# A decoder trunk on one core: sums of x in the first v pass, gate weights loaded during the second, gate bias added by VectorE, and other slots between the stages

## The chip, the core and the metric

The kernel runs on one core of a Trainium2 chip. Its engines are TensorE (PE; its weight loads are shown as PEld), VectorE (DVE), ScalarE (ACT), GpSimd (POOL) and SyncE (SP), which here only issues transfers. Each engine takes its instructions in program order, and semaphores order them between engines. The metric is the device time of one execution in microseconds (us), as the median of several.

## The reference, cut to what matters

One layer of a decoder trunk on x of 512 tokens by 2048 features, in float32:

```python
h = x @ w_in + b_in      # columns: [FoX q,k,v,z,forget | SWA q,k,v,z | MoBA q,k,v,z | gates fox,swa,moba]
# A: attention with a running sum of log_sigmoid(forget), 8 heads of 64
# B: sliding-window attention, window 128, a learned sink per head
# C: attention to the own block of 256 and the best past blocks
branch_i = (heads_i * silu(z_i)) @ w_branch_i           # 512 -> 2048, for A, B and C
y   = sum_i sigmoid(gate_i) * branch_i                  # three gates of 2048 columns each
out = layer_norm(alpha * x + y @ w_out)
```

## The kernel before, in words

Every matrix product is made of three TensorE products of reduced-precision parts: an operand is split into `hi` (a rounded copy, by ACT) and `lo` (the rest, `raw - hi`, by DVE; the helper `split` or `lower`), and hi*hi, lo*hi and hi*lo are summed in PSUM. Weights come by transfer from SP into `raw` tiles, are split two steps ahead of their matmuls, and there are three pairs of `hi` and `lo`. DVE and ACT do this for every step, in one order with everything else that the program gives them.

The order of all work is the order in which the program is written. The stages follow each other on PE:

1. The v projection (`v_step`, L234): two passes of 16 steps over x's 16 row blocks, each step 12 matmuls of 324 columns, into the PSUM tiles `va` and `vc`. In the first pass each x block is loaded (`load_x`) and split into `xh` and `xl`, which stay in SBUF. `v_evac` adds the bias `vb` and stores the result to `v_rows`.
2. For the gates, `x_sums` forms for eight pairs of x blocks four sums each on POOL (`s1raw`, `xsum`); `x_sums_split` and `s1_split` split them into `sh`/`sl` and into a part of `xh`/`xl`.
3. The gate projection: six groups (three gates, two halves each) by a fast scheme of seven products instead of eight. A group has 56 steps (seven products of eight), `gate_step` (L333), each six matmuls of 512 columns into `alpha`, `beta` and `gamma`, two tiles of each. The weights are four quarters a, b, c and d, four blocks each; the dictionary `LOADS` says at which step of a group the next group's blocks are asked for, and `COMBINE` at which step DVE adds or subtracts quarters in place (`rawb = rawc - rawb`, and so on). `gate_post` takes the sums out of PSUM; its `finish` adds the gate's bias on POOL, and the sigmoid and the store to `gate_tiles` follow three steps later.
4. The h projection: steps of 12 matmuls (L727 to L729), for q, k and z of the heads, with the attention's work put between the steps by `at(i, order, f)`: f is run in step i, sorted by `order`. Before the first head, `v_split` splits v from `v_rows`, `forget_bias` forms the log-sigmoid terms (`t0` to `pair`) from `flog`, and `running_sum` sums them on PE (`csum`). `q_lower` (L548) takes a q tile from PSUM. `nsink` is the negated sink, from `sinkc`.
5. The branch products `br` (L859) of the split head outputs `ozh`/`ozl` (`split_oz`), the product with the gates, the transposes `yt` (`turn_y`, L888), the output product `o` (L918 to L920) and the layer norm. `late_gate` and `late_silu` take the last z tiles from PSUM.

The places in the first v pass and the attention that the change moves are these, before:

```python
        if KD - 1 <= n < KD + 7:
            pend[n] = x_sums(n - KD + 1)
...
    for st in range(4):
        for ps in range(2):
            at(st, 3, v_split, ps, st, fox_dests[ps])
    nl = {}
    at(4, 4, lambda: nl.update(n=forget_bias()))
    at(6, 8, lambda: running_sum(nl["n"]))
```

Of the kernel before, what the change touches and what calls it, by code (L numbers as in the profile page):

```python
# [87 lines left out]
def hybrid_kernel(ctx: ExitStack, tc: tile.TileContext, a: dict, out: bass.AP):  # L88
# [155 lines left out]
    for n in range(2):  # L244
        prepare_v(n)
    pend = {}
    gate_loads = {}
    for n in range(2 * KD):
        if n + 4 < KD:
            load_x(n + 4)  # L250
        if n % 2 == 0 and n // 2 + 3 < KD:
            load_v(n // 2 + 3)
        if n + 2 < 2 * KD:
            prepare_v(n + 2)
        if n == KD:
            vacc[1] = [att_tile(f"vc{i}") for i in range(4)]
        if KD - 1 <= n < KD + 7:
            pend[n] = x_sums(n - KD + 1)
        v_step(n)
        if KD <= n < KD + 8:  # L260
            x_sums_split(n - KD, pend[n - 1])
        if n >= KD + 2 and n % 2 == 0:
            s1_split((n - KD - 2) // 2)
        if KD + 1 <= n < KD + 5:
            v_evac(0, n - KD - 1)
    x_ctx.close()


    rawp = gate_ctx.enter_context(tc.tile_pool(name="rawp", bufs=4))
    raw_of = {}  # L270

    def load_gate(sc, q, blk):
        if sc >= len(GROUPS):
# [6 lines left out]
        nc.sync.dma_start(r, a["wa"][(sc * 4 + "abcd".index(q)) * 4 + blk])  # L280
# [66 lines left out]
    def finish(sc, t, i, n, u):

        b, half = GROUPS[sc]
        nc.gpsimd.tensor_tensor(out=t, in0=t, in1=evs[sc, "bias", n], op=ALU.add)  # L350
# [7 lines left out]
    def gate_post(sc, m):

        out = []  # L360
        if m == 6:
            for n in range(2):
                evs[sc, "bias", n] = post.tile([P, S], F32, tag="bias", name="gbias")
                nc.gpsimd.dma_start(evs[sc, "bias", n], a["bg"][2 * sc + n:2 * sc + n + 1].to_broadcast([P, S]))
        elif m in (7, 8):
            u = m - 7
            nc.scalar.activation(post_tile(sc, "p1", "p", u), bank(sc, "alpha", u), AF.Copy)
        elif m in (15, 16):
            u = m - 15
            nc.vector.tensor_add(post_tile(sc, "u2", "u", u), bank(sc, "beta", u), evs[sc, "p1", u])  # L370
        elif m in (23, 24):
            u = m - 23
            nc.scalar.activation(post_tile(sc, "c11", "c", u), bank(sc, "alpha", u), AF.Copy)
            out.append(finish(sc, evs[sc, "c11", u], 0, 0, u))
        elif m in (31, 32):
            u = m - 31
            nc.vector.tensor_add(post_tile(sc, "u3", "c", u), bank(sc, "beta", u), evs[sc, "p1", u])
        elif m in (39, 40):
            u = m - 39
            t = evs[sc, "u3", u]  # L380
            nc.vector.tensor_add(t, bank(sc, "gamma", u), t)
            out.append(finish(sc, t, 1, 1, u))
        elif m in (47, 48):
            u = m - 47
            t = evs[sc, "p1", u]
            nc.vector.tensor_add(t, bank(sc, "beta", u), t)
            out.append(finish(sc, t, 1, 0, u))
        elif m in (55, 56):
            u = m - 55
            t = evs[sc, "u2", u]  # L390
            nc.vector.tensor_add(t, bank(sc, "gamma", u), t)
            out.append(finish(sc, t, 0, 1, u))
        return out
# [32 lines left out]
    gate_ahead(0)  # L426
    gate_ahead(1)
    for n in range(items):
# [7 lines left out]
        for f in later.pop(n, ()):
            f()
        if m == 0 and sc:
            later.setdefault(n + 3, []).extend(gate_post(sc - 1, 56))
        later.setdefault(n + 3, []).extend(gate_post(sc, m))  # L440
# [5 lines left out]
    tail = gate_post(len(GROUPS) - 1, 56)  # L446
    for n in sorted(later):
        for f in later[n]:
            f()
    for f in tail:  # L450
        f()
    gate_ctx.close()


    ozy = ctx.enter_context(tc.tile_pool(name="ozy", bufs=12))
# [1 line left out]
    work = att_ctx.enter_context(tc.tile_pool(name="work", bufs=2))
    const = att_ctx.enter_context(tc.tile_pool(name="const", bufs=1))
    flog = const.tile([P, 4, NH], F32, name="flog")
    vfox = const.tile([P, 4, NH, P], F32R, tag="v", name="vfox")  # L460
    vswa = const.tile([P, 4, 2, P], F32R, name="vswa")
    sinkc = const.tile([P, NH], F32, name="sinkc")
    nsink = const.tile([P, NH], F32, name="nsink")
    vld = [work.tile([P, 4, NV], F32, tag="pth", name=f"vld{j}") for j in range(2)]
    for j in range(2):
        nc.sync.dma_start(vld[j], a["vs"][j])
    nc.gpsimd.dma_start(sinkc, a["sinks"].to_broadcast([P, NH]))
# [639 lines left out]
```

## Time and profile before

| | |
|---|---|
| median of three runs | 1398.51 us (1398.47 to 1399.36) |
| the profiled execution | 1399.42 us |
| its span in the profile | 1397.7 us |
| granted TensorE clock, mean | 0.984 |
| PE busy | 1343.8 us (96%) |
| DVE busy | 925.2 us (66%) |
| ACT busy | 655.7 us (47%) |
| POOL busy | 264.2 us (19%) |
| moved by DMA | 174.97 MB, mean 125 GB/s |

The span is that of the profiled execution; 1.7 us of its time lie outside it. The clock is the share of full speed that the chip granted to PE; where PE has waited, the profile shows stretches of half clock. A list of waits gives, for an engine and a line, what it waited for. `L` numbers are those of the kernel before.

### The profile page before, as it was taken

What the parts mean: (1) busy time and instruction counts of PE and PEld (TensorE: products, weight loads), DVE (VectorE), ACT (ScalarE), POOL (GpSimd) and SP (SyncE); (2) the same over time, 40 slices, a digit from 0 to 9 for tenths busy, and PEclk for the clock granted to TensorE, in tenths of its full rate; (3) what the DMA queues carried; (4) which work ended last, traced back from release to release, by engine and by line L of the source; (5) the groups of instructions that cost most, each with busy time, mean ns of one, the idle gap of its engine ahead of it and who ended that gap; (6) DMA issues with size and microseconds to landing.
All of it is one profiled execution on the core that took longest, in us unless ns stands there. A gap on an engine that the chain in (4) does not pass through costs nothing.

```text
span 1397.7 us, 18535 instructions
## 1 busy us (share of the span) xinstructions
PE 1343.8 (96%) x6435; PEld 1122.3 (80%) x6435; DVE 925.2 (66%) x1591; ACT 655.7 (47%) x1202; POOL 264.2 (19%) x300
## 2 busy tenths in 40 slices
PE   8889999999999999899999999999998999999994
PEld 7868788787878788688888998888887888888884
DVE  5758888898888888556666556555645666533348
ACT  4435555455555555456655555565653222222231
POOL 3601311122121311212122323121220000000006
PEclk9899999999999999999999999999999999999998
DMA  7271707153351703342222222222224555543223
GB/s 234 84 274 41 259 33 260 42 212 105 128 188 37 261 34 101 135 121 85 97 91 78 82 76 91 76 76 91 76 76 166 181 181 181 191 170 105 91 76 120
DMA packets 57822, 174.97 MB, mean 125 GB/s; under 512 B 6568, under 2 KB 8104, under 8 KB 56960
## 3 DMA queue, kind: packets, MB, share of 16 engines
q1 hardware_dynamic: 47680, 150.07, 32.3%
q10 hardware_dynamic: 8064, 13.91, 2.6%
q0 software_dynamic: 1984, 9.81, 2.2%
q8 instruction: 50, 0.82, 0.2%
q14 instruction: 44, 0.36, 0.1%
HBM read 155.64 MB, written 18.12 MB: 124 GB/s over the span
## 4 chain that ended last, share of the span: by engine, by line
PE 82%; DVE 7%; issue 4%; DMA 3%; POOL 1%; ACT 1%; SPq 0%; DVEq 0%; ACTq 0%; POOLq 0%
PE h L727 9%; PE h L729 9%; PE h L728 8%; PE br L859 8%; PE beta L341 4%; PE o L918 4%; PE o L919 4%; PE o L920 4%; PE beta L339 4%; PE beta L340 4%; PE alpha L341 3%; PE gamma L339 3%; PE gamma L340 3%; PE gamma L341 3%; DVE glo L116 2%
## 5 line engine op out<-in xcount | busy, mean ns | idle before, releaser
L144 ACT ACTIVATE hi<-raw 128x512 fp32r<-128x512 f32 x252 | 158.8, 631 | 334.8 <-PE o L919 107.0
L147 DVE TENSOR_TENSOR lo<-raw,hi 128x512 fp32r<-128x512 f32 x252 | 177.4, 707 | 170.4 <-ACT hi L144 140.1
L727 PE MATMUL h<-xh,hi 128*128 128x512 f32 x528 | 208.9, 396 | 3.9 <-ACT hi L144 3.9
L729 PE MATMUL h<-xh,lo 128*128 128x512 f32 x528 | 207.4, 393 | 2.0 <-DVE lo L147 2.0
L728 PE MATMUL h<-xl,hi 128*128 128x512 f32 x528 | 206.7, 391 | 0.0
L643 POOL TENSOR_SCALAR lt<-lt,st 128x128 f32<-128x128 f32 (+2 forms) x96 | 71.2, 741 | 295.7 <-DVE st L642 293.8
L729 PEld LDWEIGHTS h<-xh,lo 128*128 128x128 f32 x528 | 99.5, 188 | 24.9 <-DVE lo L147 3.3
L727 PEld LDWEIGHTS h<-xh,hi 128*128 128x128 f32 x528 | 99.5, 189 | 22.7 <-ACT hi L144 4.3
L728 PEld LDWEIGHTS h<-xl,hi 128*128 128x128 f32 x528 | 99.7, 189 | 18.8
L116 DVE TENSOR_TENSOR glo<-rawd,ghi 128x512 fp32r<-128x512 f32 x96 | 74.8, 779 | 33.1 <-ACT ghi L115 27.6
L115 ACT ACTIVATE ghi<-rawa 128x512 fp32r<-128x512 f32 x96 | 59.2, 630 | 68.7 <-DVE rawa L308 29.0
L115 ACT ACTIVATE ghi<-rawd 128x512 fp32r<-128x512 f32 x96 | 60.7, 633 | 63.2 <-DVE glo L116 37.7
L918 PE MATMUL o<-hi,yh 128*128 128x512 f32 (+1 forms) x232 | 88.9, 383 | 0.7 <-DVE z L924 0.7
L919 PE MATMUL o<-hi,yl 128*128 128x512 f32 (+1 forms) x232 | 88.6, 382 | 0.0
L341 PE MATMUL alpha<-glo,xh 128*128 128x512 f32 x192 | 77.6, 404 | 11.4 <-DVE glo L116 10.7
L115 ACT ACTIVATE ghi<-rawb 128x512 fp32r<-128x512 f32 x96 | 60.6, 633 | 59.5 <-PE beta L340 23.7
L920 PE MATMUL o<-lo,yh 128*128 128x512 f32 (+1 forms) x232 | 88.6, 382 | 0.0
L116 DVE TENSOR_TENSOR glo<-rawb,ghi 128x512 fp32r<-128x512 f32 x96 | 75.9, 821 | 8.0 <-PE alpha L340 4.0
L859 PE MATMUL br<-hi,ozh 128*128 128x512 f32 x192 | 76.3, 398 | 4.5 <-ACT ozh L115 4.5
L341 PE MATMUL beta<-glo,sh 128*128 128x512 f32 x192 | 76.1, 396 | 1.2 <-DVE glo L116 1.2
L339 PE MATMUL alpha<-ghi,xh 128*128 128x512 f32 x192 | 76.2, 397 | 1.0 <-ACT ghi L115 1.0
L340 PE MATMUL alpha<-ghi,xl 128*128 128x512 f32 x192 | 75.8, 395 | 0.0
(229 smaller groups left out, 3191.3 us busy)
## 6 DMA issues: line engine op xcount, KB each, us to landing
raw<-in_ws SPq DMA_DIRECT2D x130, 512.0 KB, 3.5
rawc<-in_wa SPq DMA_DIRECT2D x25, 512.0 KB, 4.4
rawa<-in_wa SPq DMA_DIRECT2D x24, 512.0 KB, 5.0
rawb<-in_wa SPq DMA_DIRECT2D x24, 512.0 KB, 5.8
rawd<-in_wa SPq DMA_DIRECT2D x24, 512.0 KB, 5.4
sig<-gate_tiles SPq DMA_DIRECT2D x48, 256.0 KB, 3.9
gate_tiles<-u ACTq DMA_DIRECT2D x24, 256.0 KB, 4.0
rawv<-in_wv SPq DMA_DIRECT2D x15, 324.0 KB, 3.1
```

The lines of the kernel that those rows point to most:

```text
L115: nc.scalar.activation(hi, raw, AF.Copy)
L116: nc.vector.tensor_sub(lo, raw, hi.bitcast(F32))
L144: nc.scalar.activation(hi, raw, AF.Copy)
L147: nc.vector.tensor_sub(lo, raw, hi.bitcast(F32))
L339: nc.tensor.matmul(o, sth[:, us], hi, start=first, stop=False, skip_group_check=True)
L340: nc.tensor.matmul(o, stl[:, us], hi, start=False, stop=False, skip_group_check=True)
L341: nc.tensor.matmul(o, sth[:, us], lo, start=False, stop=last, skip_group_check=True)
L727: nc.tensor.matmul(accs[t], hi[:, cc], xh[:, k], start=(k == 0), stop=False)
L728: nc.tensor.matmul(accs[t], hi[:, cc], xl[:, k], start=False, stop=False)
L729: nc.tensor.matmul(accs[t], lo[:, cc], xh[:, k], start=False, stop=(k == KD - 1))
L859: nc.tensor.matmul(bracc[g, st], o[:, 4 * b + kt, ss], w, start=(kt == 0 and n == 0), stop=(kt == 3 and n == 2))
L918: nc.tensor.matmul(o, yb["h"][:, k, sl], hi, start=(k == 0), stop=False)
```

## The change

- `x_sums` moves from steps 15 to 22 into steps 2 to 16 of the v projection, one at every second step; its tile comes from the pool of the a quarters, the ring of x buffers has 8 instead of 16, and the `sl` splits go to steps 9 to 26.
- The broadcast of `vb` moves from the start to step 5; v stores follow one step after their additions; the warm-up's PSUM tile comes from another ring.
- The first group's quarters b, a and c are asked for from step 17 to step 30 (the last c by `LOADS` in the first gate step), d when x's buffers are given back. The first combine and the first two preparations of gate weights happen in steps 29 to 31.
- In the groups, the combines of b move two steps ahead (into the group before, for the first), those of a one step ahead, those of d three steps later, and the loads of a three steps later. The bias is no longer added on POOL: DVE adds it, in eight additions for each half tile instead of five, and ACT makes one copy less. The table `AFTER` says when. The bias broadcast moves from step 6 of its group to step 52 of the group before.
- The last group's last additions and stores move into h steps 0 to 2. The attention's pools are opened in step 2, `flog` comes by its own transfer from `v_rows`, `v_split` moves to steps 7 to 10, `forget_bias` is cut in two parts at orders 6 of steps 4 and 5, `nsink` moves to step 12. The first three weight loads of h move to steps 51 to 55 of the last group.
- The last `late_silu` moves from order 4 to 3, ahead of `split_oz`, one `split_oz` three steps later, and the transposes one weight step later, their PSUM tiles being opened earlier.

```diff
-        xraw[k] = xin.tile([P, S], F32, tag="x", name="xraw", bufs=16)
+        xraw[k] = xin.tile([P, S], F32, tag="x", name="xraw", bufs=8)
...
-    for j in range(2):
-        nc.gpsimd.dma_start(vb[j], a["bv"][j:j + 1].to_broadcast([P, NV]))
...
-        COMBINE[2 * blk] = ("b", "c", "b", blk, ALU.subtract)
-        COMBINE[7 + 2 * blk] = ("a", "b", "a", blk, ALU.add)
+        COMBINE[(2 * blk - 2) % 56] = ("b", "c", "b", blk, ALU.subtract)
+        COMBINE[6 + 2 * blk] = ("a", "b", "a", blk, ALU.add)
         COMBINE[26 + 2 * blk] = ("b", "c", "a", blk, ALU.subtract)
-        COMBINE[35 + 2 * blk] = ("d", "d", "a", blk, ALU.subtract)
+        COMBINE[38 + 2 * blk] = ("d", "d", "a", blk, ALU.subtract)
...
-        LOADS.setdefault(36 + 2 * blk, []).append(("a", blk))
+        LOADS.setdefault(39 + 2 * blk, []).append(("a", blk))
...
-        nc.gpsimd.tensor_tensor(out=t, in0=t, in1=evs[sc, "bias", n], op=ALU.add)
...
+    def add_bank(sc, out, tag, name, other, u):
+        t = tile_of(sc, out, tag, u)
+        nc.vector.tensor_add(t, bank(sc, name, u), evs[sc, "bias", other] if isinstance(other, int) else
+                             evs[sc, other, u])
...
+    def bias_p1(sc, u):
+        nc.vector.tensor_add(evs[sc, "p1", u], evs[sc, "p1", u], evs[sc, "bias", 0])
...
+    for u, (m1, m2, m3, m4, m5, m6, m7, m8) in enumerate(
+            [(11, 17, 20, 32, 43, 45, 48, 57), (13, 19, 21, 34, 46, 51, 50, 59)]):
+        after(9 + u, copy_p1, u)
+        after(m1, add_bank, "q1", "q", "alpha", 1, u)
+        after(m2, add_bank, "u2", "u", "beta", "q1", u)
+        after(m3, bias_p1, u)
+        after(m4, add_bank, "q1", "q", "beta", "q1", u)
+        after(m5, add_bank, "q1", "q", "gamma", "q1", u)
+        after(m5 + 2, finish, "q1", 1, 1, u)
+        after(m6, add_bank, "c11", "c", "alpha", 0, u)
+        after(m6 + 2, finish, "c11", 0, 0, u)
+        after(m7, add_bank, "p1", "p", "beta", "p1", u)
+        after(m7 + 2, finish, "p1", 1, 0, u)
+        after(m8, add_bank, "u2", "u", "gamma", "u2", u)
+        after(m8 + 2, finish, "u2", 0, 1, u)
...
-    gate_ahead(0)
-    gate_ahead(1)
+    begin = {}
+    for blk in range(4):
+        begin[17 + blk] = ("b", blk)
+        begin[(22, 23, 25, 27)[blk]] = ("a", blk)
+        begin[26 + 2 * blk] = ("c", blk)
+    stores = []
+    x_done = [9, 11, 14, 16, 19, 21, 24, 26]
+    for n in range(2 * KD):
...
+        if n in begin:
+            load_gate(0, *begin[n])
+        if n == 29:
+            combine(0, *COMBINE[54])
+        if n + 2 < 2 * KD:
+            prepare_v(n + 2)
+        else:
+            gate_ahead(n + 2 - 2 * KD)
+        if n == 5:
+            for j in range(2):
+                nc.gpsimd.dma_start(vb[j], a["bv"][j:j + 1].to_broadcast([P, NV]))
...
+        if n >= 2 and n % 2 == 0 and n < 18:
+            x_sums(n // 2 - 1)
+        v_step(n)
...
+        if n in x_done:
+            x_sums_split(x_done.index(n))
...
+        if m == 52 and sc + 1 < len(GROUPS):
+            gate_bias(sc + 1)
...
+        for ps in range(2):
+            nc.gpsimd.dma_start(flog[:, :, 4 * ps:4 * ps + 4], a["vs"][ps, :, :, 320:])
...
-        evac(t + p, zm[p], *(ZL if p < 3 else ((0, 3, late_gate), (0, 4, late_silu))))
+        evac(t + p, zm[p], *(ZL if p < 3 else ((0, 3, late_gate), (0, 3, late_silu))))
...
-                    at(i + 1 + dt // 2, 8, turn_y, g // 3, dt)
+                    at(i + 2 + dt // 2, 8, turn_y, g // 3, dt)
...
+    at(2, 9, open_attention)
...
-            at(st, 3, v_split, ps, st, fox_dests[ps])
+            at(7 + st, 3, v_split, ps, st, dests[ps])
...
-    at(4, 4, lambda: nl.update(n=forget_bias()))
-    at(6, 8, lambda: running_sum(nl["n"]))
+    at(4, 6, lambda: (nl.append(forget_bias()), next(nl[0])))
+    at(5, 6, lambda: nl.append(next(nl[0])))
+    at(6, 8, lambda: running_sum(nl[1]))
+    at(12, 7, lambda: nc.vector.tensor_scalar(nsink, sinkc, -1.0, None, op0=ALU.mult))
```

What stands where on DVE, at three places. First, the end of the first v pass before. `xl` and `lo` belong to x blocks and v weights, `sl` to the sums; the numbers behind the names tell tiles apart.

```order
L116 TENSOR_TENSOR xl_63<-xraw_343,xh_62 128x512
L116 TENSOR_TENSOR lo_406<-rawv_303,hi_405 128x324
L116 TENSOR_TENSOR xl_63<-xraw_365,xh_62 128x512
L116 TENSOR_TENSOR lo_426<-rawv_345,hi_425 128x324
L116 TENSOR_TENSOR lo_442<-rawv_345,hi_441 128x324
L116 TENSOR_TENSOR lo_466<-rawv_385,hi_465 128x324
L116 TENSOR_TENSOR sl_80<-xsum_446,sh_79 128x768
L116 TENSOR_TENSOR lo_493<-rawv_385,hi_492 128x324
```

The first `sl` came after all x blocks. Now, from the same engine, a stretch of the first pass:

```order
L117 TENSOR_TENSOR xl_63<-xraw_301,xh_62 128x512
L117 TENSOR_TENSOR sl_83<-xsum_187,sh_82 128x768
L117 TENSOR_TENSOR lo_375<-rawv_275,hi_374 128x324
L117 TENSOR_TENSOR xl_63<-xraw_321,xh_62 128x512
L117 TENSOR_TENSOR lo_401<-rawv_275,hi_400 128x324
L117 TENSOR_TENSOR xl_63<-xraw_348,xh_62 128x512
L117 TENSOR_TENSOR sl_83<-xsum_234,sh_82 128x768
L117 TENSOR_TENSOR lo_423<-rawv_323,hi_422 128x324
L117 TENSOR_TENSOR xl_63<-xraw_370,xh_62 128x512
```

The splits of the sums stand between those of x and of the weights.

Second, the attention's opening on DVE, before: the end of the chain of `forget_bias`, which leads from `t0` over `t2` and `nlf` to `pair`, and behind it the two `qs` of `q_lower`.

```order
L514 TENSOR_TENSOR t2_5000<-t2_5000,t0_4998 128x32
L515 TENSOR_SCALAR t1_4999<-flog_4845 128x32
L516 TENSOR_TENSOR nlf_4997<-t2_5000,t1_4999 128x32
L521 TENSOR_TENSOR pair_5023<-nlf_4997,pair_5023 128x4x8
L548 SCALAR_TENSOR_TENSOR qs_4990<-h0_4876,bT_61,qs_4990 64x512
L548 SCALAR_TENSOR_TENSOR qs_4992<-h0_4876,bT_61,qs_4992 64x512
L147 TENSOR_TENSOR lo_5028<-raw_4807,hi_5027 128x512
```

Now the first part of that chain:

```order
L148 TENSOR_TENSOR lo_4922<-raw_4786,hi_4921 128x512
L520 SCALAR_TENSOR_TENSOR t0_4945<-flog_4876 128x32
L522 TENSOR_SCALAR t1_4946<-t0_4945 128x32
L523 RECIPROCAL t1_4946<-t1_4946 128x32
L524 TENSOR_TENSOR t0_4945<-t0_4945,t1_4946 128x32
L525 TENSOR_TENSOR t1_4946<-t0_4945 128x32
L526 TENSOR_SCALAR t2_4947<-t1_4946 128x32
L562 SCALAR_TENSOR_TENSOR qs_4937<-h0_4807,bT_61,qs_4937 64x512
L562 SCALAR_TENSOR_TENSOR qs_4939<-h0_4807,bT_61,qs_4939 64x512
L148 TENSOR_TENSOR lo_4956<-raw_4786,hi_4955 128x512
L529 TENSOR_TENSOR t2_4947<-t2_4947,t1_4946 128x32
```

Both `qs` and a `lo` of the h weights stand between the chain's two parts.

Third, the opening of the branch products on DVE, before, with `sg` the last silu and `ozl` the lower parts of the head outputs.

```order
L147 TENSOR_TENSOR lo_9803<-raw_9627,hi_9802 128x512
L116 TENSOR_TENSOR ozl_9782<-ot_7173,ozh_9781 128x512
L116 TENSOR_TENSOR ozl_9782<-ot_7517,ozh_9781 128x512
L116 TENSOR_TENSOR ozl_9782<-ot_7882,ozh_9781 128x512
L116 TENSOR_TENSOR ozl_9782<-ot_8167,ozh_9781 128x512
L583 SCALAR_TENSOR_TENSOR sg_9818<-h32_9713,bT_61,sg_9818 128x512
L147 TENSOR_TENSOR lo_9835<-raw_9691,hi_9834 128x512
```

And now:

```order
L148 TENSOR_TENSOR lo_9775<-raw_9599,hi_9774 128x512
L597 SCALAR_TENSOR_TENSOR sg_9790<-h32_9685,bT_61,sg_9790 128x512
L117 TENSOR_TENSOR ozl_9754<-ot_7145,ozh_9753 128x512
L117 TENSOR_TENSOR ozl_9754<-ot_7489,ozh_9753 128x512
L117 TENSOR_TENSOR ozl_9754<-ot_7854,ozh_9753 128x512
L117 TENSOR_TENSOR ozl_9754<-ot_8139,ozh_9753 128x512
L148 TENSOR_TENSOR lo_9809<-raw_9663,hi_9808 128x512
```

The last silu now stands ahead of the four `ozl`, and `lo` follows behind them.

More of the change, by code (lines that the diff above doesn't have):

```diff
@@ L242, in v_step @@
             nc.tensor.matmul(o, xh[:, k, lx], wl, start=False, stop=(k == KD - 1))
[L244 to L269, printed above, removed]
     raw_of = {}
@@ L358, in gate_post @@
[L358 to L393, printed above, removed]
@@ L395, in hybrid_kernel, with gate_bias, tile_of @@
-    for q in "abcd":
-        for blk in range(4):
-            load_gate(0, q, blk)
+    def gate_bias(sc):
+        for n in range(2):
+            evs[sc, "bias", n] = post.tile([P, S], F32, tag="bias", name="gbias")
+            nc.gpsimd.dma_start(evs[sc, "bias", n], a["bg"][2 * sc + n:2 * sc + n + 1].to_broadcast([P, S]))
+    def tile_of(sc, name, tag, u):
+        if (sc, name, u) not in evs:
+            evs[sc, name, u] = post.tile([P, S], F32, tag=tag, name=name, bufs=1 if tag == "c" else 2)
+        return evs[sc, name, u]
@@ L417, in gate_ahead @@
         sc, m = divmod(n, 56)
-        if m in COMBINE:
-            combine(sc, *COMBINE[m])
+        if m in COMBINE and sc + (m == 54) < len(GROUPS):
+            combine(sc + (m == 54), *COMBINE[m])
         gate_prepare(n)
+        if sc == len(GROUPS) - 1 and m in (51, 53, 55):
+            load((m - 51) // 2)
         for q, blk in LOADS.get(m, ()):
@@ L431, in hybrid_kernel @@
         gate_step(n)
-        if n < 4:
-            v_evac(1, n)
+        for f in stores:
+            f()
+        stores = [v_evac(1, n)] if n < 4 else []
         if n == 0:
             s1_split(7)
[L436 to L440, printed above, removed]
+        if n == 4:
+            gate_bias(0)
+        if m == 52 and sc + 1 < len(GROUPS):
+            gate_bias(sc + 1)
+        for g, d in ((sc - 1, m + 56), (sc, m)):
+            for f, args in AFTER.get(d, ()) if g >= 0 else ():
+                f(g, *args)
         if sc == len(GROUPS) - 1:
@@ L445, in hybrid_kernel @@
                 x_back((m - 50) // 2)
[L446 to L455, printed above, removed]
-    att_ctx = ExitStack()
[L457 to L467, printed above, removed]
-    nc.vector.tensor_scalar(nsink, sinkc, -1.0, None, op0=ALU.mult)
-    ones = work.tile([P, S], F32, tag="L", name="ones", bufs=3)
@@ L486, in v_split @@
     def v_split(ps, st, dests):
         raw = vld[ps][:, st]
-        for dst, h0, nh, c0 in dests:
-            if dst is flog:
-                nc.gpsimd.tensor_copy(flog[:, st, h0:h0 + nh], raw[:, c0:c0 + nh])
-                continue
+        for name, h0, nh, c0 in dests:
+            dst = {"fox": vfox, "swa": vswa}[name]
             r = raw[:, c0:c0 + HD * nh].rearrange("p (h d) -> p h d", d=HD)
@@ L785, in hybrid_kernel @@
         evac(t + 2, z, *Z)
-        plan_pair("fox", p, where["h", t + 1] + 3 + 4, 1.5, q, k, z, vfox)
+        plan_pair("fox", p, where["h", t + 1] + 3 + 4, 1.5, q, k, z, lambda: vfox)
         t += 3
@@ L1005, in open_psum @@
         box["psum"] = ctx.enter_context(tc.tile_pool(name="psum2", bufs=1, space=PS))
+        box["yt"] = [box["psum"].tile([P, S], F32, tag="yt", name="yt", bufs=2) for _ in range(2)]
     at(b0 - 1, 9, open_psum)
```

124 lines of the change are left out of this document (81 added, 43 removed).

## The prediction

> **What bounds the kernel now.** I read the page first, its busy line and the shares of the chain that ended last.
>
> ```profile
> PE 1343.8 (96%) x6435; PEld 1122.3 (80%) x6435; DVE 925.2 (66%) x1591; ACT 655.7 (47%) x1202; POOL 264.2 (19%) x300
> PE 82%; DVE 7%; issue 4%; DMA 3%; POOL 1%; ACT 1%; SPq 0%; DVEq 0%; ACTq 0%; POOLq 0%
> ```
>
> TensorE is busy 96% of the span, and the change neither adds nor takes a matmul. So the time can only move in two places: where PE waits, and where it works at a lower granted clock. The second view is the list of PE's waits (engine, line, what it waited for: total us, times, longest).
>
> ```profile
> PE alpha L341 <- DVE glo L116: 10.7, 6, 5.7
> PE br L859 <- ACT ozh L115: 4.5, 1, 4.5
> PE va L240 <- ACT xh L115: 4.5, 1, 4.5
> PE h L727 <- ACT hi L144: 3.9, 1, 3.9
> PE h L729 <- DVE lo L147: 2.0, 2, 1.1
> PE beta L341 <- DVE glo L116: 1.2, 6, 0.2
> PE alpha L339 <- ACT ghi L115: 1.0, 2, 0.7
> PE yt L888 <- DVE y L878: 1.0, 4, 0.3
> ```
>
> They lie at stage openings and at group boundaries. The third view takes these places as windows: from and to, length, then busy us and instruction count of PE, PEld, DVE, ACT and POOL, the granted clock, the DMA share, GB/s. Length times one minus the clock is what the clock cost.
>
> ```profile
> 5.00:9.00 4.00, 2.12 (x12) 1.74 (x12) 1.13 (x4) 0.25 (x1) 0.00 (x0) 1.00 0.88 199
> 40.50:78.50 38.00, 34.14 (x195) 31.56 (x194) 25.41 (x33) 15.79 (x31) 22.81 (x24) 0.87 0.45 154
> 49.50:63.30 13.80, 10.44 (x37) 8.55 (x38) 10.87 (x12) 5.80 (x11) 13.49 (x16) 0.63 0.26 84
> 78.50:98.00 19.50, 12.80 (x40) 8.80 (x40) 11.59 (x17) 3.98 (x7) 0.54 (x1) 0.82 0.81 313
> 565.00:585.00 20.00, 15.02 (x56) 11.25 (x56) 9.31 (x30) 9.06 (x21) 4.45 (x16) 0.91 0.46 159
> 1056.00:1070.00 14.00, 9.46 (x31) 7.28 (x31) 7.94 (x11) 6.50 (x12) 1.65 (x1) 0.76 0.39 125
> ```
>
> The second v pass (40.5 to 78.5) is the longest loss: POOL is busy 22.8 us in it, and in 49.5 to 63.3 PE runs at 0.63. There the chain passes through POOL's sums of x.
>
> **The change, part by part.** The sum is made against the profiled execution, 1399.42 us, which lies 0.91 above the median of the three runs, 1398.51.
>
> *Start and first pass.* The bias broadcast leaves the start and x's sums enter the first pass.
>
> ```profile
> 2.19 8.68 DMA xraw<-in_xT
> vb<-in_bv POOLq DMA_DIRECT2D x2, 162.0 KB, 7.2
> 26.42 0.31 PE L240 MATMUL va<-hi,xh 128*128 128x324 f32 x1
> 40.50 0.31 PE L240 MATMUL vc<-hi,xh 128*128 128x324 f32 x1
> L116 DVE TENSOR_TENSOR xl<-xraw,xh 128x512 fp32r<-128x512 f32 x11 | 7.6, 688 | 0.2
> L116 DVE TENSOR_TENSOR lo<-rawv,hi 128x324 fp32r<-128x324 f32 x12 | 5.9, 495 | 6.1 <-ACT hi L115 5.6 <-DMA xraw<-in_xT 0.5
> L116 DVE TENSOR_TENSOR xl<-xraw,xh 128x512 fp32r<-128x512 f32 x3 | 3.6, 1190 | 0.0
> L116 DVE TENSOR_TENSOR lo<-rawv,hi 128x324 fp32r<-128x324 f32 x7 | 6.7, 950 | 4.0 <-ACT hi L115 3.9
> 66.50 0.97 DVE sl L116
> ```
>
> The second x block lands at 10.87, while both broadcasts are under way and only 199 GB/s move; without them I estimate it at about 5.5, which would save the whole 4.5-us wait. The rows at 26.42 and 40.50 are eight steps apart: 1.76 us a step. But DVE now has a rival there: beside POOL's sums xl takes 1.19 instead of 0.69, lo 0.95 instead of 0.495, so a POOL instruction costs DVE about 0.5. From 5.5 on, DVE needs 15 steps of 0.495 + 0.688 (17.7 us), three sl of 0.97 (2.9) and 0.5 for each of 24 POOL instructions (six sums of four, 12.0): 32.6 us, against 15 x 1.76 = 26.4 for PE. The second pass would start near 39 instead of 40.5: gain 1.5. Bounds: if every instruction finds POOL idle, 5.9 + 28.2 = 34, gain 6.5; if POOL costs its whole duration, -3.8 (rival B). x's ring has half the buffers, so SP holds back block 8 and, behind it, weights until POOL has done with blocks 0 and 1; block 15 waits for the fourth sum, by about 23, and lands five later, as it is wanted near 29. That is inside these bounds.
>
> *Second pass.* Seven of the eight sums are gone from it. Its floor is 16 x 1.76 = 28.2 us. DVE has 16 lo (7.9), five sl (4.9), eight small splits (about 4), four evacuations (about 2) and one combine (1.2), 20 us in all, so PE sets the end. I take 28.6 instead of 38.0: gain 9.4, bounds 7 (one late sum and its half clock stay) and 9.8.
>
> *Gate start.* Before, PE waits 5.7 and 1.0 us there and loses 19.5 x 0.18 = 3.5 by the clock, for the c weights, loaded only when the pass is over. Now eleven of the first twelve gate blocks are asked for at steps 17 to 30 and the first c at 26, three steps (5.3 us) ahead of its use. Eleven times 0.512 MB and four v blocks of 0.324 are 7 MB in about 25 us, 280 GB/s, below the 313 that this window carried. Of 10.2 I leave 0.6: gain 9.6, bounds 8 and 10.2.
>
> *Groups.* At each of the boundaries DVE's combine and glo lie beside POOL's bias additions.
>
> ```profile
> 155.74 3.39 SPq L280 DMA_DIRECT2D rawc<-in_wa  x2
> rawc<-in_wa SPq DMA_DIRECT2D x25, 512.0 KB, 4.4
> 163.79 1.22 DVE L308 TENSOR_TENSOR rawb<-rawc,rawb 128x1024 f32<-128x1024 f32 x1
> 167.27 2.20 POOL L350 TENSOR_TENSOR u<-u,gbias 128x512 f32<-128x512 f32 x1 [7.34 <-DVE u L391]
> 168.24 1.78 DVE L116 TENSOR_TENSOR glo<-rawa,ghi 128x512 fp32r<-128x512 f32 x1
> 170.54 0.67 DVE L116 TENSOR_TENSOR glo<-rawa,ghi 128x512 fp32r<-128x512 f32 x1
> ```
>
> Next to one of 2.20, glo takes 1.78, and 0.67 alone. With POOL out, the five later alpha waits (10.7 - 5.7 = 5.0) and the six beta waits (1.2) lose their cause: 6.2. DVE gets six more additions of about 0.7 a group (ACT two fewer copies), 4 us in a group of some 79 in which DVE is about two thirds busy: hidden, as long as no combine stands behind a late transfer. That is the price: the first c block is asked for at 155.74 and lands at about 160.1; its combine moves two steps (2.7 us) ahead, from 163.79 to 161. About 1 us of slack stays at the combine, and the first product that needs it comes two steps later. The bias broadcast and stores now lie beside these loads. I leave 2.2 us for late ones: gain 4.0, bounds -6 (rival C) and 6.2.
>
> *Attention opening.*
>
> ```profile
> 567.06 0.17 DVE L468 TENSOR_SCALAR nsink<-sinkc 128x8 f32<-128x8 f32 x1 [5.05 <-DMA sinkc<-in_sinks]
> 572.06 0.47 ACT L493 ACTIVATE vfox<-vld 128x320 fp32r<-128x320 f32 x1 [6.24 <-DMA vld<-v_rows]
> 580.33 0.18 DVE L504 SCALAR_TENSOR_TENSOR t<-flog 128x32 f32<-128x32 f32 x1
> 587.32 0.19 DVE L521 TENSOR_TENSOR pair<-nlf,pair 128x32 fp32r<-128x32 f32 x1 [0.36 <-ACT pair L520]
> 587.54 1.51 DVE L548 SCALAR_TENSOR_TENSOR qs<-h,bT,qs 64x512 fp32r<-64x512 f32 x2
> ```
>
> nsink and vfox keep ACT and DVE waiting for transfers while hi and lo queue behind them. They cost 3.9 (h L727), 2.0 (h L729, its two places both here), 0.2 of issue and 20 x 0.09 = 1.8 by the clock: 7.9. nsink goes to step 12, the v splits to steps 7 to 10, and both waits go. What is late next is the running sum's chain: pair was ready at 587.5, just when csum wanted it. Now both qs (1.51) and one lo (0.67) stand inside that chain, and it starts about 0.2 later: csum waits 2.4 us. With 1.3 for the clock and other openings that is 3.7 kept, so gain 4.2, bounds 1.5 (a late flog transfer as well) and 7.
>
> *Mix opening.*
>
> ```profile
> 1057.14 0.69 ACT L577 ACTIVATE sg<-h,bT 128x512 f32<-128x512 f32 x1 [2.31 <-PE h L729]
> 1060.79 0.74 DVE L583 SCALAR_TENSOR_TENSOR sg<-h,bT,sg 128x512 f32<-128x512 f32 x1
> ```
>
> The first br takes a PSUM bank that the last silu reads. That silu stands behind four ozl splits and ends at 1061.5; br began at 1061.64 after 4.5 us, and the window loses 14 x 0.24 = 3.4 more. Now it follows the gate: 1057.83 + 0.74, with a wait of about 1.6 and 0.6 of clock. Of 7.9, gain 5.7, bounds 4 and 6.5. The four ozl are behind it, and br's later matmuls want them over 12 steps.
>
> *Transposes* one weight step later: 1.0 of waits, gain 1.0, bounds 0.5 and 1. The last group's additions and stores now lie in the first three h steps; h's first matmuls take hi and lo past them on DVE (two additions of about 0.7), covered by the two-step lead of 5.5 us.
>
> Sum: 1.5 + 9.4 + 9.6 + 4.0 + 4.2 + 5.7 + 1.0 = 35.4, so 1399.4 - 35.4 = 1364.0, or 1363.1 on the median's scale. I say 1364.
>
> **A rule on the clock.** The Trainium skill (TensorE: Matmul & The Clock Gate, section "HAM oscillation — how this bites in real kernels") asks for no idle gaps of PE above about 3.4 us. This trace differs: no wait in 49.5 to 63.3 exceeds 1.3 us, and the clock there is 0.63. By that rule the two short waits that I leave would cost no clock, and the sum would come to about 1362.
>
> **The rivals.**
> A, as summed: 1357 to 1371, chance 0.56.
> B, POOL blocks DVE in the first pass. For it speaks that in 49.5 to 63.3 POOL's work and PE's low clock go together; against it, the 0.5 above. If an instruction of POOL costs DVE its 0.72 or more, 24 x 0.22 = 5.3 is lost there: 1369; with a half clock of some 4 us as in the second pass before, 1373. Range 1369 to 1376, chance 0.16. The Trainium skill (SBUF — State Buffer, section "Who interferes with whom") states an exclusive lock between DVE and GpSimd, which would be this case; the longer DVE rows agree that they contend, not that the whole duration is lost.
> C, c weights land late at five boundaries by 2 to 3 us each: 5 x 2 to 3 = 10 to 15 in place of the gain of 4: 1376 to 1383, chance 0.11.
> D, the other side: they are late by as much as x's second block was at the start, 4.5 us and more, for the same reason (broadcasts beside loads). Each boundary then waits about 4 and loses 3.4 at half clock, as 14 x 0.24 in the mix window; 7.4 x 5 = 37 takes all of the gain elsewhere (31.4) and 5 more: 1405. It decides from 6.3 us a boundary. Against it, four c blocks and the two broadcasts of 0.256 MB are spread over eight steps of about 1.4 us, 2.6 MB in 11 us or 230 GB/s, under the 313 that the gate's start carried. Chance 0.05, and 0.02 for ending within 0.2%.
> E, the moved gate loads don't come early, since SP's queue holds them behind x or v loads that wait for buffers: the 9.6 stays out, 1373, chance 0.04.
> F, the sums hide entirely and csum's wait, too, is small: 5 + 2.5 better, 1352 to 1357, chance 0.06.
>
> **How the numbers follow.** A difference under 0.2% (2.8 us) can't be told from no change with this kernel. All cases but D end far below 1395.7: faster 0.93, within 0.2% 0.02, slower 0.05. The range reaches from F to C's middle, 1354 to 1380, and leaves out about 0.15. A's own is 1357 to 1371.
>
> **What the changed profile would show.** The second v pass starting near 39 and lasting under 29.5 us; no alpha wait above 1 us at the gate start; in the groups, glo of 0.7 everywhere and POOL idle; PE waiting for csum 2 to 3 us; br's first wait under 2. The prediction is wrong if DVE's xl or sl in the first pass runs above 1.2 us on average, if PE's waits name a combine or glo behind rawc in every group, or if granted clock falls below 0.9 in a window of the first pass.

## The result, and the profile after

The change takes the kernel from 1398.93 us (median of four runs, 1398.47 to 1400.64) to 1355.39 us (median of four, 1353.25 to 1356.5): a ratio of 0.9685 with a 95% interval from 0.9668 to 0.9701. That is 43.5 us; 35 were forecast. The profiled execution took 1356.5 us with a span of 1354.7, so the spans differ by 43.0, and the accounts below are made on these two spans.

The busy line and the shares of the chain, on the page of the changed kernel:

```profile
PE 1325.1 (98%) x6435; PEld 1116.5 (82%) x6435; DVE 911.9 (67%) x1627; ACT 650.3 (48%) x1190; POOL 179.5 (13%) x246
PE 94%; DVE 4%; issue 1%; DMA 1%; ACT 0%; DVEq 0%; SPq 0%
```

PE's instructions are as many as before, and 94% of the chain is now PE's own work instead of 82%. POOL has 54 instructions fewer, DVE 36 more, and yet DVE is busy 13 us less: its instructions are shorter where no POOL instruction lies beside them.

The four longest entries in the list of PE's waits after:

```profile
PE alpha L314 <- DVE glo L117: 2.7, 3, 1.7
PE csum L544 <- issue: 2.4, 1, 2.4
PE va L239 <- DVE xl L117: 1.8, 3, 1.3
PE br L869 <- DVE sg L597: 1.6, 1, 1.6
```

The windows of the places shown before (from and to, length, busy us of PE, PEld, DVE, ACT, POOL, granted clock, DMA share, GB/s): the start, the second v pass, the gate's first group, a later group, the attention's and the mix's opening.

```profile
5.00:9.00 4.00, 2.88 (x16) 2.38 (x16) 1.60 (x4) 1.01 (x2) 1.75 (x3) 1.00 0.96 335
39.55:67.92 28.37, 28.37 (x195) 28.37 (x193) 21.31 (x37) 13.75 (x28) 7.20 (x8) 1.00 0.88 298
67.92:147.26 79.34, 77.09 (x339) 62.84 (x337) 64.71 (x90) 41.02 (x67) 1.61 (x3) 1.00 0.46 157
300.66:376.82 76.16, 76.16 (x338) 63.06 (x336) 64.96 (x89) 40.56 (x67) 1.07 (x2) 1.00 0.42 144
537.00:557.00 20.00, 17.65 (x73) 14.27 (x72) 10.75 (x34) 7.99 (x16) 3.58 (x8) 0.91 0.39 137
1018.00:1032.00 14.00, 12.44 (x55) 9.99 (x54) 10.71 (x17) 8.14 (x15) 1.68 (x1) 1.00 0.55 192
```

The second v pass is PE alone, 28.37 us without a gap or a slow clock. So is a later group, 76.16 us. The same two groups before:

```profile
78.47:166.62 88.15, 81.19 (x339) 64.44 (x337) 69.13 (x89) 41.65 (x69) 11.28 (x7) 0.96 0.52 184
324.04:402.77 78.73, 77.38 (x337) 62.77 (x336) 67.66 (x83) 41.46 (x69) 15.66 (x10) 1.00 0.41 141
```

From the starts of the stages in the two traces, the account by stage is this. The forecast's terms stand beside it.

| stage | before | after | gained | forecast |
|---|---|---|---|---|
| to the second v pass | 40.50 | 39.55 | 0.95 | 1.5 |
| second v pass | 37.97 | 28.37 | 9.6 | 9.4 |
| six groups, to h's first matmul | 482.24 | 461.64 | 20.6 | 9.6 + 4.0 |
| h to br (both openings' waits) | 500.93 | 493.26 | 7.7 | 4.2 + 2.9 of 5.7 |
| br to the last matmul | 318.31 | 314.08 | 4.2 | 2.8 of 5.7 + 1.0 |
| after the last matmul | 17.74 | 17.82 | -0.1 | 0 |

The stages gained 7.6 us more than the sum of 35.4; 7.0 of them lie in one row, the six groups with their start.

The starts of the products part this row. A group has seven products, and one without a hold-up takes 10.88 us. The first product of the first group took 22.08 us before and 13.72 after, so 8.4 us were gained at the gate's start. POOL adds no bias in it, since no group came before. The other 12.2 us belong to the groups: 11.8 to the five later ones and 0.45 to the rest of the first. A later group before lost 1.77 us in its first product and 0.80 in its fourth.

### The profile page after: what moved, and what is told of

It is laid out like the page before. It is cut to its first block, busy times and chain, and to the rows that moved or that the text cites. A ratio compares the mean times of both kernels' runs of the same rounds, so it can differ in the third digit from the quotient of the medians.

```text
span 1354.7 us, 18432 instructions
## 1 busy us (share of the span) xinstructions
PE 1325.1 (98%) x6435; PEld 1116.5 (82%) x6435; DVE 911.9 (67%) x1627; ACT 650.3 (48%) x1190; POOL 179.5 (13%) x246
## 4 chain that ended last, share of the span: by engine, by line
PE 94%; DVE 4%; issue 1%; DMA 1%; ACT 0%; DVEq 0%; SPq 0%
PE br L869 10%; PE h L741 9%; PE h L743 9%; PE h L742 9%; PE beta L314 5%; PE beta L312 5%; PE beta L313 5%; PE o L928 4%; PE o L929 4%; PE o L930 4%; PE gamma L314 3%; PE gamma L312 3%; PE gamma L313 3%; PE alpha L314 3%; PE alpha L312 3%; PE alpha L313 3%
## 5 line engine op out<-in xcount | busy, mean ns | idle before, releaser
L117 DVE TENSOR_TENSOR glo<-rawd,ghi 128x512 fp32r<-128x512 f32 x96 | 66.3, 691 | 27.3 <-ACT ghi L116 25.0
L117 DVE TENSOR_TENSOR glo<-rawb,ghi 128x512 fp32r<-128x512 f32 x96 | 66.2, 690 | 18.9 <-ACT ghi L116 17.7
L869 PE MATMUL br<-lo,ozh 128*128 128x512 f32 x192 | 74.8, 390 | 0.0
L869 PE MATMUL br<-hi,ozl 128*128 128x512 f32 x192 | 74.7, 389 | 0.0
```

Source lines behind the costliest of these rows:

```text
L869: nc.tensor.matmul(bracc[g, st], o[:, 4 * b + kt, ss], w, start=(kt == 0 and n == 0), stop=(kt == 3 and n == 2))
```

## The experiments

All compare with the changed kernel's 1355.39 and its trace. Single executions are named so; the changed kernel's own runs lie up to 2.1 us from their median. The kernel before, run again beside the experiments, took 1399.8 to 1400.4 us, 0.9 to 1.4 more than beside the result. In the profiles, the second v pass began anywhere between 38.4 and 39.8 in kernels with the same start. So stages are compared, not only times.

**POOL adds the gate bias again.**

```diff
-        after(m1, add_bank, "q1", "q", "alpha", 1, u)
-        after(m2, add_bank, "u2", "u", "beta", "q1", u)
-        after(m3, bias_p1, u)
-        after(m4, add_bank, "q1", "q", "beta", "q1", u)
+        after(m2, add_bank, "u2", "u", "beta", "p1", u)
+        after(m4, add_bank, "q1", "q", "beta", "p1", u)
...
+        after(m5, pool_bias, "q1", 1, u)
-        after(m6, add_bank, "c11", "c", "alpha", 0, u)
+        after(m6, copy_c11, u)
+        after(m6, pool_bias, "c11", 0, u)
...
+        after(m7, pool_bias, "p1", 0, u)
...
+        after(m8, pool_bias, "u2", 1, u)
```

> The changed kernel, but POOL adds the gate bias again (48 additions, 128x512) and DVE has five additions a half tile as before; the new combine and load slots stay, and the bias broadcast stands in step 4 of its own group, since POOL's last additions read the old one until step 3. Theory 1 (POOL's additions beside DVE's two-input instructions made glo and the combines late): the groups' period goes from 76.2 back to about 77.5 to 78.7 us, glo near 1.8 us beside an addition, and waits of alpha or beta for glo return; the kernel takes 1362 to 1369. Rival (the combines and loads at other slots gave it): the period stays at 76.2 and the kernel within 2 us of 1355.

Measured: 1380.66 us (median of four; 0.986 of before, 0.9843 to 0.9876), 25 us above the changed kernel. A window of one group, and PE's waits:

```profile
310.68:391.07 80.39, 77.68 (x337) 62.61 (x336) 67.35 (x83) 41.75 (x69) 16.23 (x10) 1.00 0.40 138
PE gamma L314 <- DVE glo L117: 13.7, 13, 2.3
PE alpha L312 <- ACT ghi L116: 2.3, 5, 0.7
PE alpha L314 <- DVE glo L117: 1.6, 5, 0.5
```

POOL's additions cost 4.2 us a group here, more than either end of what was expected: the period is longer than before the change. The mechanism held, its size did not. The loss now sits in a group's last product (2.95 us) and first (1.28). In the last product two additions come back to back beside a combine of b, which now stands two steps earlier, and combine and glo take 2.31 and 1.76 us there. In the timelines of DVE and POOL:

```profile
304.23 2.31 DVE L281 TENSOR_TENSOR rawb<-rawc,rawb 128x1024 f32<-128x1024 f32 x1
306.46 1.76 DVE L117 TENSOR_TENSOR glo<-rawc,ghi 128x512 fp32r<-128x512 f32 x1
305.41 2.26 POOL L347 TENSOR_TENSOR c<-c,gbias 128x512 f32<-128x512 f32 x1
```

**The combines at their old slots, DVE keeping the bias.**

```diff
-        COMBINE[(2 * blk - 2) % 56] = ("b", "c", "b", blk, ALU.subtract)
-        COMBINE[6 + 2 * blk] = ("a", "b", "a", blk, ALU.add)
+        COMBINE[2 * blk] = ("b", "c", "b", blk, ALU.subtract)
+        COMBINE[7 + 2 * blk] = ("a", "b", "a", blk, ALU.add)
```

> The changed kernel, but the combines of b and a at their old slots (steps 0, 2, 4, 6 and 7, 9, 11, 13 of their own group); DVE keeps the bias. Theory 1: a period of 76.2 to 76.7, as without POOL each combine costs DVE 1.2 us and fits its slot. Rival (the slots gave the gain): about 77.5 or more, with alpha waiting for glo about 1 us in each group.

Measured, one execution: 1353.88 us, and the group's window

```profile
298.12:374.28 76.16, 76.16 (x337) 63.08 (x336) 64.88 (x89) 40.22 (x67) 1.07 (x2) 1.00 0.42 146
```

So the combines' new slots give nothing. They may even cost: the six groups take 459.54 us with the old ones against 461.64. Of this, 1.1 us is the second group (76.16 instead of 77.24), which no longer waits for a c block. The other 1.0 is the first group, which takes 77.8 to 79.5 us in kernels with the new slots and says little.

**Both as before.** POOL's bias and the old combine slots of b and a together, to see whether 78.7 comes back.

```diff
+        after(m5, pool_bias, "q1", 1, u)
...
+        COMBINE[2 * blk] = ("b", "c", "b", blk, ALU.subtract)
+        COMBINE[7 + 2 * blk] = ("a", "b", "a", blk, ALU.add)
```

> The changed kernel with POOL adding the gate bias again and the combines of b and a at their old slots too (the bias broadcast in step 4 of its own group). Theory: POOL's additions alone make the old period, so 78.2 to 79.0 us a group with alpha waiting about 1 us for glo, below the 80.4 of the run in which POOL added the bias at the new slots; the kernel about 1368 to 1372. Rival (the old slots do not suit the other moved work): 80 us or more.

Measured, one execution: 1378.07 us, with periods of 79.8 to 80.4. That is nearer to the rival. POOL's additions cost 3.7 to 4.3 us a group here, where the kernel before lost 2.6. Three things still differ from it: the slots of DVE's sums (`AFTER`), the combines of d and the loads of a. Which of them makes the difference was not tried. What stands is the comparison at equal slots: without POOL's additions 76.16, with them 80.4.

**The first group's loads placed after the pass.** They go to SP in the program's order b, a, c, d, after the v loop.

```diff
-        if n in begin:
-            load_gate(0, *begin[n])
-        if n == 29:
-            combine(0, *COMBINE[54])
...
+    for q in "bacd":
+        for blk in range(4):
+            if (q, blk) != ("c", 3):
+                load_gate(0, q, blk)
+    combine(0, *COMBINE[54])
+    gate_ahead(0)
+    gate_ahead(1)
```

> The changed kernel, but the first group's weights are asked for only after the second v pass, as before, in the order b, a, c, d, and its first combine and two preparations stand there too. Theory: the wait at the gate's start comes back, 5 to 9 us of it and 3.4 us at half clock, so 1364 to 1368. Rival (the transfers were not the cause, the full DVE was): 1357 or less.

Measured, one execution: 1357.42 us; the first group's window and SP's issues in the timeline (start, us, engine, line):

```profile
67.56:150.40 82.84, 78.99 (x338) 63.90 (x337) 68.78 (x95) 41.02 (x67) 1.61 (x3) 0.98 0.47 165
50.80 2.42 SPq L253 DMA_DIRECT2D rawb<-in_wa  x4
59.50 1.38 SPq L253 DMA_DIRECT2D rawc<-in_wa  x3
```

The first group is 3.5 us longer, with one wait of 3.4 us where 5 to 9 and a half clock were expected; the time lies between theory and rival. The loads placed "late" are issued from 50.8 on, 17 us ahead of the gate: SP had nothing else to do and ran ahead to them, since their buffers were free. But they come in one burst, and the first combine waits for c until 68.39.

**The same loads held back.** So the next kernel gives SP something to wait for: a small transfer of the `lo` tile of v step 26 ahead of them, and the old order a, b, c, d.

```diff
+        if n == 24:
+            nc.sync.dma_start(a["scratch"][:, :NV], vparts[26][1][:NH, :NV].bitcast(F32))
...
+    for q in "abcd":
```

> The changed kernel, but SP is held ahead of the first group's loads by a small transfer of the lo tile of v step 26, so that the loads begin about 11 us before the gate's first step, as they did before the change, in the order a, b, c, d; the first combine and two preparations come after the pass. Theory (what counts is when SP can issue the loads, that is when buffers are free, not the place in the program): the wait of 5 to 6 us and a half-clock stretch return at the gate's start, the first group lasts 87 to 89 us instead of 79.3, and the kernel takes 1363 to 1366. Rival (with POOL out of the way the start is short anyway): the first group stays below 84 us, as it did when the loads were only placed later.

Measured, one execution: 1363.02 us. The loads were issued from 55.4 on, 12.8 us ahead of the gate (11.0 before the change). The longest wait of PE, the first group's window and the issues of c:

```profile
PE alpha L314 <- DVE glo L117: 6.0, 2, 5.7
68.17:153.60 85.43, 79.66 (x339) 65.02 (x337) 68.72 (x95) 41.02 (x67) 1.61 (x3) 0.96 0.50 174
63.26 1.52 SPq L253 DMA_DIRECT2D rawc<-in_wa  x3
```

The wait of 5.7 and the clock of 0.96 of the kernel before are back. The group is 6.1 us longer than after the change, 1.6 below the expected range. So this edit gives back 6.0 of the 8.4 us of the gate's start: 3.5 came with the last kernel already, and 2.5 more with the hold and the other order, which no run here parts. What goes with the loss is when c lands. The first combine, which waits for it, before the change, with the loads placed late, and with the loads held:

```profile
82.92 1.23 DVE L308 TENSOR_TENSOR rawb<-rawc,rawb 128x1024 f32<-128x1024 f32 x1 [8.43 <-DMA rawc<-in_wa]
68.39 2.50 DVE L281 TENSOR_TENSOR rawb<-rawc,rawb 128x1024 f32<-128x1024 f32 x2 [4.80 <-DMA rawc<-in_wa]
71.31 2.51 DVE L281 TENSOR_TENSOR rawb<-rawc,rawb 128x1024 f32<-128x1024 f32 x2 [7.12 <-DMA rawc<-in_wa]
```

These are 4.4, 0.8 and 3.1 us after the gate's first matmul, and the first product takes 22.1, 17.2 and 19.8 us. In the changed kernel it is 5.4 us ahead, and the product takes 13.7. In the kernel before, the first of these loads was issued here, when the sums of x in the second pass had given their memory back:

```profile
67.48 2.15 SPq L280 DMA_DIRECT2D rawa<-in_wa  x4
```

Now the buffers of b exist from the start and those of a are free when the sums, moved into the first pass, are split.

**POOL writes zeros instead of the sums.**

```diff
-        nc.gpsimd.tensor_tensor(out=s1, in0=e[:, hi2], in1=o[:, hi2], op=ALU.add)
...
+        nc.gpsimd.memset(s1, 0.0)
+        nc.gpsimd.memset(t, 0.0)
```

> The changed kernel, but POOL writes zeros into the sums of x with two memsets instead of four additions; the sums themselves are left out. Theory (each POOL instruction with two inputs costs DVE about 0.5 us, and DVE bounds the first pass at 2.1 us a step): lo about 0.5 and xl about 0.69, steps of 1.76 us, the second pass starting at 34 to 36 instead of 39.6, the kernel 4 to 5 us faster, about 1351. Rival (transfers or ACT bound the first pass): a start of 38 to 39.6 as now.

Measured, one execution: 1351.08 us; the second pass starts at 36.20. DVE's groups in the first pass (busy us, mean ns), first of the changed kernel, then without the sums:

```profile
L117 DVE TENSOR_TENSOR xl<-xraw,xh 128x512 fp32r<-128x512 f32 x15 | 16.2, 1080 | 1.8 <-ACT xh L116 1.8
L117 DVE TENSOR_TENSOR lo<-rawv,hi 128x324 fp32r<-128x324 f32 x15 | 13.2, 881 | 1.3 <-ACT hi L116 1.3
```

```profile
L117 DVE TENSOR_TENSOR xl<-xraw,xh 128x512 fp32r<-128x512 f32 x15 | 10.3, 689 | 0.8 <-ACT xh L116 0.6
L117 DVE TENSOR_TENSOR lo<-rawv,hi 128x324 fp32r<-128x324 f32 x17 | 8.4, 494 | 5.8 <-ACT hi L116 5.2 <-DMA xraw<-in_xT 0.5
```

The sums cost DVE 15 x 0.39 + 15 x 0.39 = 11.7 us in these two groups, and without them the pass ends 3.35 us earlier, a little less than was expected. No run here puts the sums back into the second pass; that they made its loss is argued from the two traces.

**The vb broadcasts at the start.**

```diff
-        if n == 5:
-            for j in range(2):
-                nc.gpsimd.dma_start(vb[j], a["bv"][j:j + 1].to_broadcast([P, NV]))
...
+    for j in range(2):
+        nc.gpsimd.dma_start(vb[j], a["bv"][j:j + 1].to_broadcast([P, NV]))
```

> The changed kernel, but both broadcasts of vb are asked for at the start again. Theory (they halve the first transfers): the second x block lands near 10.9 us instead of about 7, PE waits 4 us or more there and a half-clock stretch follows, and since DVE bounds the first pass from that block on, the second pass starts 3 to 4 us later, near 43; about 1359. Rival (DVE bounds the pass from its end, so the start doesn't matter): 39.6 and 1355 as now.

Measured, one execution: 1358.85 us. The wait for x's second block is

```profile
PE va L240 <- ACT xh L116: 4.7, 1, 4.7
```

and the second pass starts at 42.77 instead of 39.55. So moving the broadcast brought 3.2 us, and moving the sums into the first pass took most of it back: together 0.95.

**The forget chain whole, ahead of qs.**

```diff
-    at(4, 6, lambda: (nl.append(forget_bias()), next(nl[0])))
-    at(5, 6, lambda: nl.append(next(nl[0])))
+    at(4, 6, lambda: (nl.append(forget_bias()), next(nl[0]), nl.append(next(nl[0]))))
```

> The changed kernel, but the chain of the forget bias stands whole at step 4, order 6, so that both qs and a lo come after it. Theory (these 2.2 us in the middle of the chain are csum's wait of 2.35): the wait is 0 to 0.2 us and the half clock behind it goes, 1.7 more, so about 1351.5; hi and lo of h may wait a few tenths. Rival (ACT's table load or a late flog makes it): a wait of 1.5 us or more stays.

Measured, one execution: 1355.99 us. The stage from h to br took 490.64 us instead of 493.26. csum's wait fell to 0.22 and no half clock followed, but a lo behind it now made PE wait 0.88:

```profile
551.03 0.82 PE L544 MATMUL csum<-tri,pair 128*128 128x512 f32 x4 [0.22 <-issue]
553.26 0.50 PE L743 MATMUL h<-xh,lo 128*128 128x512 f32 x1 [0.88 <-DVE lo L148]
```

In the changed kernel, DVE's timeline shows what stands in the chain's middle, and PE's the wait:

```profile
544.97 0.18 DVE L526 TENSOR_SCALAR t<-t 128x32 f32<-128x32 f32 x1
545.19 1.51 DVE L562 SCALAR_TENSOR_TENSOR qs<-h,bT,qs 64x512 fp32r<-64x512 f32 x2
546.74 0.69 DVE L148 TENSOR_TENSOR lo<-raw,hi 128x512 fp32r<-128x512 f32 x1
547.34 0.19 DVE L529 TENSOR_TENSOR t<-t,t 128x32 f32<-128x32 f32 x1
551.14 1.18 PE L544 MATMUL csum<-tri,pair 128*128 128x512 f32 x4 [2.35 <-issue]
```

The forecast of 1351.5 was missed. Against the changed kernel's profiled execution, 1356.5, the time fell by only 0.5: this execution lost 1.6 us in the second v pass (a wait of 0.7 in it) and 1.1 in the groups (five waits for glo), which the edit doesn't touch. The theory on csum is borne out by its stage alone.

**The last silu and the transposes as before.**

```diff
-        evac(t + p, zm[p], *(ZL if p < 3 else ((0, 3, late_gate), (0, 3, late_silu))))
+        evac(t + p, zm[p], *(ZL if p < 3 else ((0, 3, late_gate), (0, 4, late_silu))))
...
-                    at(i + 2 + dt // 2, 8, turn_y, g // 3, dt)
+                    at(i + 1 + dt // 2, 8, turn_y, g // 3, dt)
```

> The changed kernel, with two places as before, which lie in stages of their own: the last silu at order 4 behind four ozl, and the transposes one weight step earlier. Theory: br's first wait goes from 1.6 back to 4.5 us, with 3.4 lost at half clock after it, and the four yt waits come back and cost 0.25 each as listed and up to 0.4 more each in slower starts behind them; br's first matmul 3 us later, the stage from br to o 3.4 + 1.0 to 2.6 longer, together 7 to 9: 1362 to 1364. Rival (the silu was not what br waited for): br unchanged, 1356 to 1358.

Measured, one execution: 1361.94 us, at the lower end. PE's waits:

```profile
PE br L869 <- ACT ozh L116: 4.5, 1, 4.5
PE yt L898 <- DVE y L888: 1.0, 4, 0.3
```

From br to the last matmul it takes 317.53 instead of 314.08 us: 3.45, of which one stretch of half clock (3.41 us long) is 1.7, so the transposes cost 1.75 where the list says 1.0.

**What the remaining waits ask for.** The forget chain's parts one step earlier, the second pass's v outputs in two rings, the bias broadcast in step 4 of its own group, the old combine slots.

```diff
+        raw = post.tile([P, S], F32, tag="q" if not ps or st < 2 else "p", name="vout")[:, :NV]
...
+        if m == 4:
+            gate_bias(sc)
...
+    at(3, 6, lambda: (nl.append(forget_bias()), next(nl[0])))
+    at(4, 6, lambda: nl.append(next(nl[0])))
```

> The changed kernel with what its remaining waits ask for: the forget chain's parts at steps 3 and 4, the second pass's v outputs in two rings of buffers, the bias broadcast in step 4 of its own group instead of beside the c loads, and the combines of b and a at their old slots. Theory: no csum wait (2.4 and 1.7 of clock), no wait at the gate's start (about 2.8 with the slower starts), groups 0 and 1 at 76.2 (2 to 3 us): 8 to 9 us below the changed kernel, 1346 to 1348. Rival (the waits only move to the next late step): 1351 or more.

Measured: 1348.14 us (median of five, 1347.64 to 1348.56), 0.9628 of before with an interval from 0.9614 to 0.9641, which lies below the changed kernel's. This is 7.25 us less than the change, 0.1 above the range of the theory. All that PE still waits for, and the windows of the first group and the attention's opening:

```profile
PE br L865 <- DVE sg L593: 1.6, 1, 1.6
PE warm L197 <- DVE warm L194: 1.5, 1, 1.5
PE va L239 <- DVE xl L117: 1.1, 2, 0.9
PE o L924 <- DVE z L930: 0.7, 1, 0.7
67.14:143.71 76.57, 76.52 (x339) 62.98 (x337) 65.17 (x92) 40.77 (x67) 1.61 (x3) 1.00 0.48 162
531.00:551.00 20.00, 20.00 (x91) 16.59 (x90) 12.12 (x35) 11.31 (x22) 3.16 (x8) 1.00 0.44 164
```

The first group falls from 79.34 to 76.57. What made it long in the changed kernel was not a gate load: the third v output waited for the store of the first, since they share two buffers, and DVE's glo stood behind it. The mended kernel changes four things at once, so the share of each is read from the trace alone. In the changed kernel:

```profile
75.96 0.49 DVE L207 TENSOR_TENSOR vout<-vc,vb 128x324 f32<-128x324 f32 x1 [2.88 <-DMA v_rows<-vout]
```

## Why the prediction was right, and where its steps were off

The forecast was 1364 with 1354 to 1380, and 1355.39 lies in it, near its low end, but below the 1357 to 1371 of case A itself. Case A was right in its mechanisms; the time came out in the range of case F, the most favourable one, though what F named (sums hidden, a small wait for csum) did not come. That the range held is so in part luck. (Case C's sum, 1364 + 4 + 10, gives 1378 and not 1376 at its lower end.)

- Start and first pass: forecast 1.5, measured 0.95. The price of 0.5 us for each POOL instruction was right: xl, lo and sl take 12.2 us more than without the sums, beside 25 POOL instructions of about 1 us. So rival B, the whole duration lost, did not come. x's second block landed near 7.0, not 5.5, and PE still waits in the opening steps (0.8 for xh, 1.8 for xl).
- Second pass: 9.4 forecast, 9.6 measured. DVE's 20 us were 21.3, hidden.
- Gate start: 9.6 forecast, 8.4 measured, inside the bounds of 8 and 10.2. Before, the first product lost 11.2 us, not 10.2. The window's length times one minus the clock counts half clock also while PE idles: of the 6.8 us at half speed 1.0 were idle, so the clock cost 2.9, not 3.5; slower starts behind the waits cost the rest. After, 2.8 stayed and not 0.6. A wait of 1.7 took the place of the old one, by v outputs that wait for their own stores; the forecast did not name it, and its sign of no alpha wait above 1 us failed. Rival E, loads stuck behind SP's queue, did not come: c is asked for from 56.29 on, 11.6 us ahead of the gate, where before the first load of all was asked for 11.0 ahead.
- Groups: 4.0 forecast and 6.2 as the upper bound; 12.2 measured. This is the step that failed: the sum of listed waits was taken as the price. In the trace before, one such wait looks like this:

```profile
330.12 0.39 PE L340 MATMUL alpha<-ghi,xl 128*128 128x512 f32 x1
331.53 0.50 PE L341 MATMUL alpha<-glo,xh 128*128 128x512 f32 x1 [1.02 <-DVE glo L116]
331.87 0.40 PE L339 MATMUL alpha<-ghi,xh 128*128 128x512 f32 x1
```

Undisturbed, starts are 0.227 us apart, while a matmul lasts 0.39: they overlap. Here they are 1.41 and 0.34 apart. So the wait listed as 1.02 cost 1.18 + 0.11. A hold-up shorter than the overlap of 0.16 leaves no idle time. In this group two more hold-ups stand in no list: the starts at 327.49 and 363.15 come 0.28 and 0.15 late, and the ones behind them 0.11 more each. By the distances of starts that stand out, the group lost 2.4 us where the list shows 1.23, and 78.73 - 76.16 = 2.57 agrees nearly. Rival C, late c blocks, came once, 1.1 us in the second group; the mended kernel is rid of it.
- Attention: 4.2 forecast, 4.7 measured (7.67 from h to br less 2.98 for the mix's wait). csum's wait of 2.35 was forecast as 2.4, from the same row of qs and lo. The waits of h are gone; no run puts `nsink` or `v_split` back, so their part is argued from the traces.
- Mix: 5.7 forecast. The wait fell by 2.98, from 4.54 to 1.56, and no half clock follows; before, 5.2 us of br ran at half speed, 2.6 lost. Together 5.6.
- Transposes: 1.0 forecast and as upper bound; 1.6 to 1.75 measured, probably by the same error as in the groups.
- Rival D, slower by late c blocks, did not come near: the one late block cost 1.1 us where 6.3 at each boundary would have decided.

## What to carry to other kernels

Price a wait of a pipelined engine by the distances between the starts of its instructions, against the undisturbed distance, not by the idle time in a list; short hold-ups that no list shows add up in a loop. An engine with little to do can be the dear one: taking 14.6 us of work a group (15.66 to 1.07) off POOL and giving DVE more instructions made DVE faster. And for a queue that only issues transfers, ask when its buffers come free and when the data land; the place in the program alone does not tell.

## What the hardware showed that was not expected

The same wait for csum, 2.35 us, was followed by a half clock in the changed kernel and not in the kernel with the old silu and transposes, which up to that place is the same program. In all, seven of the nine kernels with this wait (2.3 to 2.7 us) show the half clock behind it.

In the trace before the change, half clock begins at 12.11, 53.07, 83.79, 575.31 and 1060.00, whole multiples of 3.413 us apart, and a stretch lasts 3.41 us or a whole multiple. So each trace can be cut into such steps, laid so that a stretch of half clock begins with one. These are the steps around the wait, one of the changed kernel and two of the other:

```profile
547.98:551.40 3.42, 1.07 (x5) 0.63 (x4) 2.36 (x14) 0.75 (x2) 0.00 (x0) 1.00 0.55 153
547.06:550.48 3.42, 2.29 (x11) 1.55 (x9) 3.01 (x14) 0.00 (x0) 0.00 (x0) 1.00 0.30 97
550.48:553.89 3.41, 2.18 (x11) 1.91 (x12) 2.10 (x8) 2.08 (x5) 0.00 (x0) 1.00 0.16 64
```

In the changed kernel the whole wait falls into one step, in which PE is busy for 1.07 us, and the next step runs at half clock. In the other kernel the end of a step cuts the wait in two, PE is busy for 2.29 and 2.18, and the clock stays. The twelve traces agree, from the first v pass to the last matmul: after a step at full clock in which PE idled for 1.84 us or more came half clock, and after one with 1.74 or less it did not. The one exception is a step with 1.65, at 49.65 in the kernel before, among many short waits. So a wait's length alone does not decide, but how it lies to these steps; no run shifted a wait on purpose to try this.

The Trainium skill (TensorE: Matmul & The Clock Gate, section "HAM oscillation — how this bites in real kernels") names gaps above about 3.4 us as what to avoid; in the changed kernel's trace a gap of 2.35 was enough, while one of 1.73 and one of 1.56 passed at full clock.
